# Seven-product output projections: block sums of the weights formed by accumulating loads, token operands formed beside plain tiles, reloads on another queue

## The chip, the cores and the metric

The kernel runs on one core of a Trainium2 chip. The metric is the device time of one execution in microseconds; lower is better. The matrix engine is called PE here, the vector engine DVE, the scalar engine ACT, GpSimd POOL and the sync engine SP. "POOLq" and "SPq" are the queues on which POOL and SP issue transfers.

## What is computed

One inference step of two layers over 576 tokens (64 of a running stream, 512 of a new one), model width 2048, everything in fp32. Layer A is chunk-band attention with 16 heads, layer B multi-head latent attention with 16 heads. The part that matters here is the end of each layer, an output projection of a gated mixer output, added to the layer's input:

```
y = x + (silu(gate) * mixer(rmsnorm(x))) @ w_out        # w_out is 2048 x 2048, one for each layer
```

## The kernel before

**Layout.** Activations lie transposed: 16 tiles of 128 channels by 576 tokens. For PE every fp32 operand is split into a high and a low part (`split`, L201 to L204: ACT casts the high part, DVE subtracts to get the low one), and a product is three matmuls (high·high, high·low, low·high), each with 288 tokens as its columns.

**Order of the work.** PE's instructions keep the order in which the program emits them. That order is made by `Order` (L42), which runs generators by rank and holds a clock of its own; a generator yields a pool name ("mm", "st", "x": PSUM slots) when it needs a slot. The other engines' instructions and the transfers are put in order by a scheduler that may take an instruction ahead of earlier ones when it reckons it ready. On the chip each engine and each queue then runs strictly in that order: an instruction that waits holds up all that is behind it. Tile pools are rings: the n-th tile of a pool takes the slot of the one `bufs` tiles before it, and waits until that one is done with.

**The output projection of a layer.** Its 16 tiles of 128 output channels are made in two ways. Tiles 0 to 3 are plain (`proj`, L232: 16 input tiles, 2 token halves, 3 matmuls each, so 96 matmuls; four weight parts of 128 x 512, each loaded and split by `wload`, L212). Tiles 0 and 1 are made together (`both`, L248) while the last head is still being finished; they fill the two "mm" slots of PSUM. Tiles 2 and 3 come after (`out_a` L823, `out_b` L1212); each begins when DVE has read tile 0 or 1 out of PSUM (L833 in layer A, L1222 in layer B), which adds the residual.

Tiles 4 to 15 are made in six pairs by `block_pairs` (L358). With two output tiles, two halves of the input channels (tiles 0 to 7, 8 to 15) and two token halves L and R, a two-by-two block product is done with seven products in place of eight. Each product has 24 matmuls (2 weight parts of 128 x 512, 4 blocks in each, 3 matmuls), so a pair has 168. Its weight is either a block or a sum of blocks, made by `block_weights` (L300): eight blocks of 128 x 512 are loaded by SP, and eight DVE instructions (L323, L326, L329, L333) form the sums; then `split`. Its token operand is one of the halves or a combination, made once for each layer by `block_operands` (L261): for each of eight j, four DVE subtractions (L287 to L293) and three splits on tiles j and j+8 of the mixer output. The fourth split, operand 4, overwrites the R half of the plain operand, so `last` (L295) makes it after the plain tiles. The order of the seven products is `1, 5, 6, 3, 7, 2, 4` (L361); after each one DVE adds it to the half tile of output that it belongs to (L391).

**Where the operands come from.** In layer A the mixer outputs `oA` are still on the chip. In layer B they were stored to `od` and are loaded again by 16 SP transfers (L1206 to L1209), into the same ring of 16 slots (`tag="o"`) that the raw weights of the pairs use afterwards (`raw_b`). `block_operands` is called as one piece before `out_a` and before `out_b`. After layer A each output tile is stored to `x1d`, its square is added to `lnb_acc` (`done_a`, L819; one buffer for the square), and layer B loads the tiles again by 16 SP transfers (L865 to L867) and splits them (L208, L209).

Of the kernel before, what the change touches and what calls it, by code (L numbers as in the profile page):

```python
# [15 lines left out]
F32 = mybir.dt.float32  # L16
F32R = mybir.dt.float32r
# [3 lines left out]
P = 128  # L21
D = 2048
KT = 16
# [95 lines left out]
def encoder(tc, xT, wa_in, wa_out, wb_in, wuq, wuk, wuqr, wuv, wb_out, kcT, vc, ckvcT, krcT, gains, rtab,  # L119
# [128 lines left out]
    def both(pss, name, ws, xs, before):  # L248
# [9 lines left out]
                yield None  # L258
        yield from gens[1]

    def block_operands(o, o2, pool, name):  # L261

        L, R = slice(0, 288), slice(288, 576)
        X = {1: [], 2: [], 3: [], 4: [], 5: [], 6: [], 7: []}
        for j in range(8):  # L270
            X[1].append([x[:, L] for x in o2[j]])
            X[2].append([x[:, L] for x in o2[j + 8]])
            X[3].append([x[:, R] for x in o2[j + 8]])

        def put(p, j, src):
            if p == 4:
                hi, lo = [x[:, R] for x in o2[j]]
            else:
                hi = pool.tile([P, 288], F32R, tag="T", bufs=48, name=f"{name}T{p}h{j}")
                lo = pool.tile([P, 288], F32R, tag="T", bufs=48, name=f"{name}T{p}l{j}")  # L280
            split(src, hi, lo)
            X[p].append((hi, lo))

        sub = ALU.subtract
        for j in range(8):
            a, b = o[j], o[j + 8]
            V.tensor_tensor(out=a[:, L], in0=a[:, R], in1=a[:, L], op=sub)  # L287
            put(5, j, a[:, L])
            V.tensor_tensor(out=a[:, R], in0=b[:, R], in1=a[:, R], op=sub)
            V.tensor_tensor(out=b[:, R], in0=b[:, R], in1=a[:, L], op=sub)  # L290
            put(6, j, b[:, R])
            put(7, j, a[:, R])
            V.tensor_tensor(out=b[:, L], in0=b[:, L], in1=b[:, R], op=sub)  # L293

        def last():  # L295
            for j in range(8):
                put(4, j, o[j + 8][:, L])
        return X, last

    def block_weights(w2d, pairs, seq, raw_tile, name):  # L300

        for m1, m2 in pairs:
            n_ = f"{name}{m1}"
            got, S = {}, {}

            def load(m, part):
                r = raw_tile(f"{n_}r{m}_{part}")
                nc.sync.dma_start(r, w2d[m * P:(m + 1) * P, part * WH:(part + 1) * WH])
                return r

            def block(i, k, c):
                key = i, k, c
                if key not in got:
                    got[key] = load((m1, m2)[i], 2 * k + c)
                return got[key]

            for p in seq:
                for c in range(2):
                    if p == 1:
                        src = block(0, 0, c)  # L320
                    elif p == 5:
                        S[c] = raw_tile(f"{n_}s{c}")
                        V.tensor_tensor(out=S[c], in0=block(1, 0, c), in1=block(1, 1, c), op=ALU.add)  # L323
                        src = S[c]
                    elif p == 6:
                        V.tensor_tensor(out=S[c], in0=S[c], in1=block(0, 0, c), op=ALU.subtract)  # L326
                        src = S[c]
                    elif p == 3:
                        V.tensor_tensor(out=S[c], in0=block(0, 1, c), in1=S[c], op=ALU.subtract)  # L329
                        src = S[c]  # L330
                    elif p == 7:
                        src = block(1, 0, c)
                        V.tensor_tensor(out=src, in0=block(0, 0, c), in1=src, op=ALU.subtract)  # L333
                    elif p == 2:
                        src = block(0, 1, c)
                    else:
                        src = block(1, 1, c)
                    hi = wp.tile([P, WH], F32R, tag="whi", bufs=WHL, name=f"{n_}p{p}{c}h")
                    lo = wp.tile([P, WH], F32R, tag="wlo", bufs=WHL, name=f"{n_}p{p}{c}l")
                    split(src, hi, lo)  # L340
                    yield hi, lo

    class Ahead:
        def __init__(self, gen, n):
# [10 lines left out]
            self.fill(self.n + 1)  # L355
            return self.got.pop(0)

    def block_pairs(w2d, X, pairs, raw_tile, residual, out_tile, done, name):  # L358

        L, R = slice(0, 288), slice(288, 576)  # L360
        seq = 1, 5, 6, 3, 7, 2, 4  # L361
        ws = Ahead(block_weights(w2d, pairs, seq, raw_tile, name), WHL - 2)
        for m1, m2 in pairs:
            n_ = f"{name}{m1}"
            x1, x2 = residual(m1), residual(m2)
            y1, y2 = out_tile(m1), out_tile(m2)
            yield "mm"
            a = ps_of("mm", n_ + "a")[:, 0, :288]
            bank = {1: a, 6: a, 7: a, 4: a}
            for p in seq:  # L370
                if p == 5:
                    yield "st"
                    bank[5] = bank[3] = ps_of("st", n_ + "c")[:, 0, :288]
                if p == 2:
                    yield "x"
                    bank[2] = ps_of("x", n_ + "b")[:, :288]
                for c in range(2):
                    hi, lo = ws.get()
                    for j in range(4):
                        s = slice(j * P, (j + 1) * P)  # L380
                        xh, xl = X[p][4 * c + j]
                        ends = c == 1 and j == 3
                        begins = p in (1, 2, 5) and c == 0 and j == 0
                        matmul(bank[p], hi[:, s], xh, begins, False, skip_group_check=True)
                        matmul(bank[p], hi[:, s], xl, False, False, skip_group_check=True)
                        matmul(bank[p], lo[:, s], xh, False, ends, skip_group_check=True)
                        yield None
                with tc.high_priority():
                    y, h_, add = {1: (y1, L, x1), 5: (y2, R, x2), 6: (y1, R, x1), 3: (y1, R, y1), 7: (y2, R, y2),
                                  2: (y1, L, y1), 4: (y2, L, x2)}[p]  # L390
                    V.tensor_tensor(out=y[:, h_], in0=bank[p], in1=add[:, h_], op=ALU.add)  # L391
                if p == 3:
                    od_.give("st", L_M)
                if p == 2:
                    od_.give("x", L_M)
            od_.give("mm", L_M)
            done(m1, y1)
            done(m2, y2)

# [400 lines left out]

    close(g_at)
    g_T, Tp = pool("blocksa", side="right")
    X, last_a = block_operands(oA, o2, Tp, "ao")
    g_ao, aop = pool("aout", side="right")

    def tpo(tag, dt, name):
# [16 lines left out]
    def out_a():  # L823
        for m in range(4):
            xr = residual_a(m)
            if m < 2:
                ps = first[m]
            else:
                yield "mm"
                ps = ps_of("mm", f"ao{m}")  # L830
                yield from proj(ps, wo, o2, N)
            x1 = tpo("x1", F32, f"x1_{m}")
            V.tensor_tensor(out=two(x1), in0=ps[:, :, :288], in1=two(xr), op=ALU.add)  # L833
            od_.give("mm", L_M)
            done_a(m, x1)
        last_a()
        yield from block_pairs(wa_out, X, [(m, m + 1) for m in range(4, KT, 2)], raw_a, residual_a,
                               lambda m: tpo("x1", F32, f"x1_{m}"), done_a, "ao")

    od_.spawn(5, out_a())  # L840
# [16 lines left out]

    def tpl(tag, dt, name):
        if tag == "raw":
            return lrp.tile([P, N], dt, tag=tag, bufs=RAWB, name=name)  # L860
# [342 lines left out]
    def done_b(m, y):  # L1203
        nc.gpsimd.dma_start(yT[m * P:(m + 1) * P, :], y)

    oB = []  # L1206
    for kt in range(KT):
        oB.append(bo.tile([P, N], F32, tag="o", bufs=16, name=f"bf{kt}"))
        nc.sync.dma_start(oB[kt], od[kt * P:(kt + 1) * P, :])  # L1209
    X, last_b = block_operands(oB, o2, bo, "bo")  # L1210

    def out_b():  # L1212
        for m in range(4):
# [12 lines left out]
        yield from block_pairs(wb_out, X, [(m, m + 1) for m in range(4, KT, 2)], raw_b, residual_b, out_tile_b,  # L1226
                               done_b, "bo")

    od_.spawn(5, out_b())
# [6 lines left out]

L_G, L_CQ, L_M, L_V, L_LN, L_HA, L_LB = 5.8, 10.0, 1.5, 5.0, 5.0, 8.0, 4.0
ATT = "t0 s2 t1 s3 o-1 t2 t3"
DIRECT, GA, WRAW, WHL, SGB, DEEP, VA = 2, 2, 3, 5, 2, 2, 2
LAT = (0, 1, 2, 3, 8, 4, 5, 6, 7, 9, 10)  # L1240
LAHEAD = 1
RAWB, SB, S1H, S2H, S3 = 7, 4, 3, 1, 1
# [84 lines left out]
```

## Time and profile before

| | us |
|---|---|
| median of 3 runs (2040.43 to 2044.78) | 2041.55 |
| the profiled execution | 2043.23 |
| its span | 2041.5 |
| PE busy (share of the span) | 1990.0 (97%) |
| DVE busy | 1350.7 (66%) |
| ACT busy | 1103.4 (54%) |
| POOL busy | 74.3 (4%) |
| transfers, mean over the span | 109 GB/s |

The profiled execution's own time is 1.7 us above its span and 1.7 us above the median of the runs. The pages of the profile give each engine's busy time, the waits with what ended them, tables by stretch, and the instructions in order of time. Matmuls overlap, so the time that one costs is read from how many start in a stretch, not from its own duration.

### The profile page before, as it was taken

The page shows a single profiled execution, that of the slowest core. Times are in us where ns is not written, and L with a number is a line of the kernel's source. Part 1 is how long each engine was busy: PE and PEld are TensorE (multiplying, and loading weights), DVE is VectorE, ACT ScalarE, POOL GpSimd, SP SyncE. Part 2 cuts the span into 40 slices and gives each one's busy share as a digit, 9 for nine tenths or more (in the row PEclk, how much of TensorE's full clock was granted, in tenths as well). Part 3 has the DMA queues.
Part 4 walks back from the last instruction along what each step waited for, and adds up shares of the span by engine and source line. Part 5 has one row for each costly group of instructions (what it writes and reads, how often), then busy time and mean ns, then how long its engine had stood idle before and what let it go on. Part 6 is the DMA issues. An engine that isn't in the chain of part 4 may idle for free.

```text
span 2041.5 us, 37543 instructions
## 1 busy us (share of the span) xinstructions
PE 1990.0 (97%) x14692; PEld 1969.5 (96%) x14692; DVE 1350.7 (66%) x2651; ACT 1103.4 (54%) x2034; POOL 74.3 (4%) x141
## 2 busy tenths in 40 slices
PE   8999999999999999999999899999999999995998
PEld 8999999999999999999999899999999999995998
DVE  7665555555555555558778648887776766676775
ACT  6654444544454445456344538986765656662332
POOL 0000000000000000000000000000000000000000
PEclk9999999999999999999999999999999999997999
DMA  7333333333333333333543535553223322355542
GB/s 210 86 84 94 90 85 90 83 85 89 86 94 89 86 90 78 83 81 101 171 145 118 183 78 147 159 167 112 82 77 98 86 82 84 87 154 196 164 138 68
DMA packets 121393, 223.38 MB, mean 109 GB/s; under 512 B 14272, under 2 KB 29264, under 8 KB 121216
## 3 DMA queue, kind: packets, MB, share of 16 engines
q1 hardware_dynamic: 109360, 181.22, 32.7%
q0 software_dynamic: 11856, 39.76, 5.5%
q8 instruction: 115, 1.88, 0.4%
q14 instruction: 62, 0.51, 0.1%
HBM read 183.92 MB, written 34.36 MB: 107 GB/s over the span
## 4 chain that ended last, share of the span: by engine, by line
PE 85%; issue 8%; DVE 3%; ACT 2%; DMA 1%; POOL 0%; POOLq 0%; SPq 0%; DVEq 0%; ACTq 0%
PE g L164 8%; PE lat L164 6%; PE u L164 3%; PE a2p L164 3%; PE a4p L164 3%; PE a14p L164 3%; PE a12p L164 3%; PE a9p L164 3%; PE a15p L164 3%; PE a11p L164 3%; PE a7p L164 3%; PE a8p L164 3%; PE a5p L164 3%; PE a10p L164 3%; PE a6p L164 3%
## 5 line engine op out<-in xcount | busy, mean ns | idle before, releaser
L204 DVE TENSOR_TENSOR wa_2l<-wa_2r,wa_2h 128x512 fp32r<-128x512 f32 x61 | 42.2, 691 | 92.2 <-ACT wa_2h L203 92.2
L203 ACT CAST wa_2h<-wa_2r 128x512 fp32r<-128x512 f32 x61 | 37.7, 619 | 103.7 <-PE a2p L164 10.1
L204 DVE TENSOR_TENSOR wa_3l<-wa_3r,wa_3h 128x512 fp32r<-128x512 f32 x61 | 42.2, 692 | 44.1 <-ACT wa_3h L203 42.6
L203 ACT CAST wa_0h<-wa_0r 128x512 fp32r<-128x512 f32 x61 | 37.8, 619 | 60.9 <-DMA wa_0r<-wa_in 5.2
L203 ACT CAST wa_3h<-wa_3r 128x512 fp32r<-128x512 f32 x61 | 37.7, 618 | 51.5 <-PE a2p L164 4.5
L204 DVE TENSOR_TENSOR wa_0l<-wa_0r,wa_0h 128x512 fp32r<-128x512 f32 x61 | 41.9, 687 | 17.0 <-ACT wa_0h L203 17.0
L203 ACT CAST wa_1h<-wa_1r 128x512 fp32r<-128x512 f32 x61 | 37.8, 620 | 23.7 <-PE a0pg L164 1.8
L204 DVE TENSOR_TENSOR wa_1l<-wa_1r,wa_1h 128x512 fp32r<-128x512 f32 x61 | 41.8, 685 | 10.5 <-ACT wa_1h L203 10.5
L164 PE MATMUL bo<-boh,wbo_0h 128*128 128x288 f32 x32 | 7.6, 323 | 22.4 <-DVE by L1222 22.4
L164 PE MATMUL u<-cqh,wq_0h 128*128 128x288 f32 x128 | 27.7, 298 | 0.5 <-ACT q6raw L478 0.3
L164 PEld LDWEIGHTS bo<-boh,wbo_0h 128*128 128x128 f32 x32 | 5.8, 214 | 22.6 <-issue 22.6
L164 PE MATMUL u<-cqh,wq_0l 128*128 128x288 f32 x128 | 27.4, 296 | 0.0
L164 PE MATMUL u<-cql,wq_0h 128*128 128x288 f32 x128 | 27.3, 295 | 0.0
L204 DVE TENSOR_TENSOR wb_1l<-wb_1r,wb_1h 128x512 fp32r<-128x512 f32 x25 | 17.2, 687 | 15.2 <-ACT wb_1h L203 15.1
L204 DVE TENSOR_TENSOR wb_3l<-wb_3r,wb_3h 128x512 fp32r<-128x512 f32 x25 | 17.2, 686 | 14.4 <-ACT wb_3h L203 14.3
L203 ACT CAST wb_3h<-wb_3r 128x512 fp32r<-128x512 f32 x25 | 15.4, 616 | 18.1 <-PE lat L164 9.6
L203 ACT CAST wb_1h<-wb_1r 128x512 fp32r<-128x512 f32 x25 | 15.5, 619 | 17.7 <-PE lat L164 8.8
L164 PE MATMUL lat<-bh,wb_0h 128*128 128x288 f32 x88 | 20.0, 311 | 4.5 <-ACT bh L208 4.5
L164 PE MATMUL g<-bh,wb_1h 128*128 128x288 f32 x112 | 24.3, 298 | 0.0
L164 PE MATMUL g<-bh,wb_0h 128*128 128x288 f32 x112 | 24.3, 298 | 0.0
L164 PE MATMUL g<-bh,wb_2h 128*128 128x288 f32 x112 | 24.3, 298 | 0.0
L164 PE MATMUL g<-bh,wb_3h 128*128 128x288 f32 x112 | 24.2, 298 | 0.0
(6782 smaller groups left out, 8051.9 us busy)
## 6 DMA issues: line engine op xcount, KB each, us to landing
wa_0r<-wa_in SPq DMA_DIRECT2D x61, 256.0 KB, 2.9
wa_1r<-wa_in SPq DMA_DIRECT2D x61, 256.0 KB, 2.9
wa_2r<-wa_in SPq DMA_DIRECT2D x61, 256.0 KB, 2.9
wa_3r<-wa_in SPq DMA_DIRECT2D x61, 256.0 KB, 2.9
wb_0r<-wb_in SPq DMA_DIRECT2D x25, 256.0 KB, 2.9
wb_1r<-wb_in SPq DMA_DIRECT2D x25, 256.0 KB, 2.9
wb_2r<-wb_in SPq DMA_DIRECT2D x25, 256.0 KB, 2.9
wb_3r<-wb_in SPq DMA_DIRECT2D x25, 256.0 KB, 2.9
```

The source lines that it names most:

```text
L164: nc.tensor.matmul(out, lhs, rhs, start=start, stop=stop, **kw)
L203: ACT.copy(hi, src)
L204: V.tensor_tensor(out=lo, in0=src, in1=hi.bitcast(F32), op=ALU.subtract)
```

## The change

Three things are edited, in both layers.

- **Weight sums by accumulating loads.** The DVE instructions that form sums of weight blocks are gone. A tile is loaded with one block by SP and another block is then added to it by a transfer on POOL's queue that accumulates into the tile (`accum_op=ALU.add`). Since transfers only add, signs move to the token operands (`neither`, a negated difference) and to the additions after the products (two are subtractions now). The order of the products is `5, 1, 2, 6, 4, 7, 3`. The tile of product 5 is kept: product 6 adds a block to it, product 3 another. A pair has ten plain loads and eight accumulating ones where it had eight plain ones. Loads are emitted three items ahead of the splits (`LOADS`). PSUM: products 1, 6 and 7 share an "mm" slot, 5 and 3 one "x" slot, 2 and 4 one each; "st" is no longer used here.
- **Token operands beside plain tiles.** `block_operands` returns a generator; `beside` takes one of its eight steps at every fourth step of the plain tiles 2 and 3. Each operand has a ring of its own of 16 slots (before: one of 48).
- **Reloads on POOL's queue.** The 16 loads of `x1d` at the start of layer B, and the 16 of `od` for layer B's operands, the latter in pairs (j, j+8) and five pairs ahead, go to POOL's queue.

```diff
+    def beside(gen, other, n):
+        for j, w in enumerate(gen):
+            yield w
+            if j % n == 0:
+                next(other, None)
...
+        def form():
+            for j in range(8):
+                a, b = o(j)
+                less(a[:, L], a[:, L], a[:, R])
+                put(5, j, a[:, L])
+                less(a[:, R], b[:, R], a[:, R])
+                put(7, j, a[:, R])
+                neither(b[:, R], b[:, R], a[:, L])
+                put(6, j, b[:, R])
+                neither(b[:, L], b[:, L], b[:, R])
+                late.append(b[:, L])
+                yield None
...
+    SEQ = 5, 1, 2, 6, 4, 7, 3
...
+                def add(t, src):
+                    nc.gpsimd.dma_start(t, src, accum_op=ALU.add)
...
+                        if p in (1, 7):
+                            nc.sync.dma_start(t, block(1, 1, c))
+                        elif p == 2:
+                            nc.sync.dma_start(t, block(1, 2, c))
+                        elif p == 4:
+                            nc.sync.dma_start(t, block(2, 2, c))
+                        elif p == 5:
+                            nc.sync.dma_start(t, block(2, 1, c))
+                        if p == 5:
+                            add(t, block(2, 2, c))
+                        elif p == 6:
+                            add(t, block(1, 1, c))
+                        elif p == 3:
+                            add(t, block(1, 2, c))
+                        elif p == 7:
+                            add(t, block(2, 1, c))
+                        yield t, n_
+        raws = Ahead(loads(), LOADS)
...
+                    if p == 7:
+                        V.tensor_tensor(out=two(y2), in0=two(y2), in1=ps[:, None, :].to_broadcast((P, 2, 288)),
+                                        op=ALU.subtract)
...
-                yield from proj(ps, wo, o2, N)
+                yield from beside(proj(ps, wo, o2, N), form_a, 4)
...
-        nc.sync.dma_start(x1, x1d[m * P:(m + 1) * P, :])
+        nc.gpsimd.dma_start(x1, x1d[m * P:(m + 1) * P, :])
...
-        nc.sync.dma_start(oB[kt], od[kt * P:(kt + 1) * P, :])
+            nc.gpsimd.dma_start(t[-1], od[kt * P:(kt + 1) * P, :])
...
-                yield from proj(ps, wo, o2, N)
+                yield from beside(proj(ps, wo, o2, N), form_b, 4)
```

## Rows read from the trace of the kernel before

**Rows 1.** The page, PE's busy tenths in 40 slices of 51 us.

```profile
PE   8999999999999999999999899999999999995998
```

**Rows 2.** Who PE waited for: us in total, times, longest; 850 to 1220, 1800 to 2042.

```profile
PE lat L164 <- ACT bh L208: 4.5, 1, 4.5
PE ao L164 <- DVE x L833: 4.3, 1, 4.3
...
PE bo L164 <- DVE by L1222: 22.4, 1, 22.4
```

**Rows 3.** DVE in order of time: start, us, instruction; ends of both layers' waits.

```profile
977.57 0.75 DVE L833 TENSOR_TENSOR x<-ao,xr 128x576 f32<-128x576 f32 x1
...
982.25 0.45 DVE L204 TENSOR_TENSOR aoT7l<-a7sg,aoT7h 128x288 fp32r<-128x288 f32 x1
...
1851.69 0.46 DVE L287 TENSOR_TENSOR bf<-bf 128x288 f32<-128x288 f32 x1 [4.00 <-DMA bf<-od]
...
1874.10 0.45 DVE L204 TENSOR_TENSOR boT5l<-bf,boT5h 128x288 fp32r<-128x288 f32 x1
1874.47 0.75 DVE L1222 TENSOR_TENSOR by<-bo,bxr 128x576 f32<-128x576 f32 x1
...
1876.17 0.44 DVE L204 TENSOR_TENSOR boT7l<-bf,boT7h 128x288 fp32r<-128x288 f32 x1
```

**Rows 4.** Stretches: busy us of each engine (instructions), PEclk, DMA share, GB/s.

```profile
core 0: us, PE busy (x) PEld busy (x) DVE busy (x) ACT busy (x) POOL busy (x), PEclk, DMA share, GB/s
...
974.00:978.00 4.00, 0.02 (x1) 0.00 (x0) 4.00 (x11) 2.45 (x7) 0.00 (x0) 0.94 0.08 28
978.00:982.00 4.00, 3.63 (x15) 3.63 (x16) 4.00 (x9) 2.34 (x5) 1.08 (x2) 0.50 0.65 205
982.00:990.00 8.00, 8.00 (x54) 8.00 (x53) 4.26 (x8) 1.24 (x2) 0.00 (x0) 0.85 0.66 211
...
1854.00:1866.00 12.00, 0.00 (x0) 0.00 (x0) 11.17 (x30) 4.39 (x12) 0.00 (x0) 0.67 1.05 393
...
1905.00:2035.00 130.00, 130.00 (x983) 130.00 (x982) 94.15 (x160) 48.04 (x78) 6.48 (x12) 1.00 0.40 120
```

**Rows 5.** PE in order of time, the first matmuls after layer B's wait.

```profile
1875.36 0.82 PE L164 MATMUL bo<-boh,wbo_0h 128*128 128x288 f32 x2 [22.44 <-DVE by L1222]
...
1880.09 0.42 PE L164 MATMUL bo<-boh,wbo_1h 128*128 128x288 f32 x2
```

**Rows 6.** SP's queue in order of time, raw weights of layer B's first pair.

```profile
1861.53 5.99 SPq L308 DMA_DIRECT2D bo4r<-wb_out  x4
...
1891.64 1.13 SPq L308 DMA_DIRECT2D bo4r<-wb_out  x2
```

**Rows 7.** Transfers by tile: queue, count, KB each, median us to landing.

```profile
bf<-od SPq DMA_DIRECT2D x16, 288.0 KB, 6.0
...
bo8r<-wb_out SPq DMA_DIRECT2D x8, 256.0 KB, 3.1
...
b15qf<-qd POOLq DMA_DIRECT2D x1, 288.0 KB, 4.1
```

**Rows 8.** The page's groups: a weight split; busy us, mean ns, idle before.

```profile
L204 DVE TENSOR_TENSOR wb_1l<-wb_1r,wb_1h 128x512 fp32r<-128x512 f32 x25 | 17.2, 687 | 15.2 <-ACT wb_1h L203 15.1
...
L203 ACT CAST wb_1h<-wb_1r 128x512 fp32r<-128x512 f32 x25 | 15.5, 619 | 17.7 <-PE lat L164 8.8
```

**Rows 9.** POOL in order of time: the store that ends a pair, two pairs of layer B.

```profile
1948.20 0.54 POOL L1204 DMA_DIRECT2D yT<-by  x1 [2.79 <-DVE by L391]
...
1970.47 0.54 POOL L1204 DMA_DIRECT2D yT<-by  x1 [2.91 <-DVE by L391]
```

**Rows 10.** ACT and DVE in order of time, between layer A's last product and layer B.

```profile
1141.95 0.68 ACT L406 ACTIVATE lnb15sq<-x 128x576 f32<-128x576 f32 x1 [2.57 <-DVE x L391]
...
1142.67 0.76 DVE L407 TENSOR_TENSOR lnb_acc<-lnb_acc,lnb15sq 128x576 f32<-128x576 f32 x1 [0.81 <-ACT lnb15sq L406]
...
1146.05 0.81 DVE L209 SCALAR_TENSOR_TENSOR bl<-bx,gn,bh 128x576 fp32r<-128x576 f32 x1
```

More of the change, by code (lines that the diff above doesn't have):

```diff
@@ L278, in put, with less @@
             else:
-                hi = pool.tile([P, 288], F32R, tag="T", bufs=48, name=f"{name}T{p}h{j}")
-                lo = pool.tile([P, 288], F32R, tag="T", bufs=48, name=f"{name}T{p}l{j}")
+                hi = pool.tile([P, 288], F32R, tag=f"T{p}", bufs=16, name=f"{name}T{p}h{j}")
+                lo = pool.tile([P, 288], F32R, tag=f"T{p}", bufs=16, name=f"{name}T{p}l{j}")
             split(src, hi, lo)
             X[p].append((hi, lo))
[L284 to L293, printed above, removed]
+        def less(out, a, b):
+            V.tensor_tensor(out=out, in0=a, in1=b, op=ALU.subtract)
@@ new lines, in neither @@
+        def neither(out, a, b):
+            V.scalar_tensor_tensor(out=out, in0=a, scalar=-1.0, in1=b, op0=ALU.mult, op1=ALU.subtract)
+        def form():
[10 more added lines that the diff above has]
+                yield None
@@ L295, in last @@
         def last():
             for j in range(8):
[L297 to L341, printed above, removed]
@@ new lines, in last, with block_weights, loads, block @@
+                put(4, j, late[j])
+        late = []
+        return X, form(), last
+    SEQ = 5, 1, 2, 6, 4, 7, 3
+    def block_weights(w2d, pairs, raw_tile, sum_tile, name):
+        def loads():
+            for m1, m2 in pairs:
+                S = {}
+                def block(i, k, c):
+                    m, part = (m1, m2)[i - 1], 2 * k - 2 + c
+                    return w2d[m * P:(m + 1) * P, part * WH:(part + 1) * WH]
+                def add(t, src):
+                    nc.gpsimd.dma_start(t, src, accum_op=ALU.add)
+                for p in SEQ:
+                    for c in range(2):
+                        n_ = f"{name}{m1}p{p}{c}"
+                        if p == 5:
+                            t = S[c] = sum_tile(n_)
+                        elif p in (6, 3):
+                            t = S[c]
+                        else:
+                            t = raw_tile(n_)
+                        if p in (1, 7):
[6 more added lines that the diff above has]
+                            nc.sync.dma_start(t, block(2, 1, c))
+                        if p == 5:
+                            add(t, block(2, 2, c))
[7 more added lines that the diff above has]
+        raws = Ahead(loads(), LOADS)
+        for _ in range(14 * len(pairs)):
+            src, n_ = raws.get()
+            hi = wp.tile([P, WH], F32R, tag="whi", bufs=WHL, name=n_ + "h")
+            lo = wp.tile([P, WH], F32R, tag="wlo", bufs=WHL, name=n_ + "l")
+            split(src, hi, lo)
+            yield hi, lo
@@ L836, in out_a @@
         last_a()
-        yield from block_pairs(wa_out, X, [(m, m + 1) for m in range(4, KT, 2)], raw_a, residual_a,
+        yield from block_pairs(wa_out, X, [(m, m + 1) for m in range(4, KT, 2)], raw_a, raw_a, residual_a,
                                lambda m: tpo("x1", F32, f"x1_{m}"), done_a, "ao")
@@ L859, in tpl @@
         if tag == "raw":
-            return lrp.tile([P, N], dt, tag=tag, bufs=RAWB, name=name)
+            return lrp.tile([P, N], dt, tag="raw", bufs=RAWB, name=name)
         bufs = {"s1": SB, "s2": SB, "s3": S3}.get(tag, 1)
@@ L1204, in done_b, with pair_b @@
         nc.gpsimd.dma_start(yT[m * P:(m + 1) * P, :], y)
-    oB = []
-    for kt in range(KT):
-        oB.append(bo.tile([P, N], F32, tag="o", bufs=16, name=f"bf{kt}"))
-        nc.sync.dma_start(oB[kt], od[kt * P:(kt + 1) * P, :])
-    X, last_b = block_operands(oB, o2, bo, "bo")
+    def pair_b(j):
+        t = []
+        for kt in (j, j + 8):
+            t.append(bo.tile([P, N], F32, tag="o", bufs=16, name=f"bf{kt}"))
+            nc.gpsimd.dma_start(t[-1], od[kt * P:(kt + 1) * P, :])
+        return t
+    oB = Ahead((pair_b(j) for j in range(8)), 5)
+    X, form_b, last_b = block_operands(lambda j: oB.get(), o2, bo, "bo")
     def out_b():
@@ L1225, in out_b @@
         last_b()
-        yield from block_pairs(wb_out, X, [(m, m + 1) for m in range(4, KT, 2)], raw_b, residual_b, out_tile_b,
+        yield from block_pairs(wb_out, X, [(m, m + 1) for m in range(4, KT, 2)], raw_b, raw_b, residual_b, out_tile_b,
                                done_b, "bo")
```

50 lines of the change are left out of this document (25 added, 25 removed).

## Prediction, made before the change was run

> **What bounds the kernel now.** I read the slices first: PE is at nine tenths or more nearly everywhere, and a stretch of slices near the end falls to five [rows 1]. A gain can therefore come only from PE's few gaps, or from fewer matmuls, and the change keeps all matmuls. The list of PE's waits gives the gaps: 4.3 us in layer A and 22.4 us in layer B, both ended by the DVE addition that reads plain tile 0 out of PSUM, and 4.5 us at the start of layer B's projections [rows 2]. The instructions in order of time say why that addition was late: DVE was running `block_operands`. In layer B its first subtraction waits for reloaded tiles and starts at 1851.7, the addition (L1222) comes at 1874.5, with only two of the piece's instructions behind it; in layer A the addition (L833) comes at 977.6 in the midst of the same work, which ends at 982.7 [rows 3]. After each gap PE runs at the lower clock: granted 0.50 in 978 to 982 and 0.85 in 982 to 990 [rows 4]. Within the pairs there is nothing to gain: 130.00 of 130 us busy, 983 matmuls, so 0.132 us each, while DVE has 36 us free [rows 4]. A change of 0.2%, about 4 us, is what a measurement of this kernel can tell from none.
>
> **The change part by part.**
>
> *Operands beside the plain tiles.* The additions L833 and L1222 are now emitted before the first step of the operands, so they no longer stand behind them; what they need is the residual and PE's result. Both gaps go: 4.3 + 22.4 = 26.7 us. With them goes the slow restart. Layer A: 69 matmuls start in 978 to 990, PE idle for 0.4 us of it; at 0.132 us the other 11.6 us hold 88, so 19 are missing, 2.5 us. Layer B: from 1875.36 to 1880.09 are 24 matmuls in 4.73 us [rows 5], against 3.2, so 1.5 us. Together 30.7 us.
>
> What is late next is DVE. A layer's operands are 8 x 7 = 56 DVE instructions, which start 0.37 us apart (1874.10 to 1874.47 [rows 3]): 20.7 us. Plain tiles 2 and 3 take PE 2 x 96 x 0.132 = 25.4 us. DVE also has to split their weights and to make two additions of some 0.67 us. In layer A the work is begun early and ends 5 us after the gap's end [rows 3], some 17 us before the first pair now: cover enough, cost 0 (2 at worst). In layer B the tiles land at about 1851 as now; POOL's queue is free to issue them when the last head is stored, and the loads run at the transfer engines' full rate, 393 GB/s at a share of 1.05 [rows 4], whichever queue issues them. 20.7 us of operands, 4 splits [rows 8] and 4 additions (some 5 us) end at about 1877, and the first pair starts at 1852.9 + 25.4 = 1878.3 (the wait that ends at 1875.36 began 22.44 us earlier [rows 5]). That just fits.
>
> *A slot in layer B's ring that is late.* `pair_b` takes slots in the order j, j+8, so the second raw weight tile (product 5, part 1) falls on the slot of tile 8, which `last` must have read first. Its read can't come before plain tile 3 is past its first step (about 1866), and perhaps only after the operands (1877). In the kernel before, the two loads with such slots were issued 30 us after the first four [rows 6]; they belonged to a late product then. Now a load (3.1 us [rows 7]), an accumulating load (4 to 5, an estimate from the 4.1 us of a plain POOL load [rows 7]) and a split (0.62 + 0.69 and a handover, 1.4 [rows 8]) follow, 9 us, and PE wants it 1.6 us into the pair, at 1880. So 0 to 6 us of waiting, and at the far end a slow restart of 1.5: I take 4.5 in all, as DVE will be full until 1877.
>
> *Weight sums by transfers.* 8 DVE instructions for each pair go; in the pairs DVE isn't the bound [rows 4], so they give 0. Eight loads become ten, and eight accumulating ones come in. No row shows one. Its cost to the engines: at least a plain load, 256 KB at 393 GB/s = 0.67 us; at most, I say, three passes (load, read the tile, write it through), 2.0 us. A pair takes 1970.47 - 1948.20 = 22.27 us [rows 9]. Ten plain loads and four residuals and outputs of 288 KB are 3.80 MB, 9.7 us. That leaves 12.6 us for eight, 1.57 us each. At one pass the engines are at 68%, at two (1.33 us) at 92%, at three at 115%. I take two passes, a load plus a read of the tile, which lies midway: hidden, cost 0; ends 0 and +41 us (12 pairs x 8 x 0.43). A gain is excluded, as PE has no gap in the pairs.
>
> By the Trainium skill (Collectives: The Full Stack, The bandwidth ceiling: the fold count and why AG ≠ RS ≠ AR) an add in a transfer is slower than a copy because it reads two sources, about half the rate. No run here shows it yet; by it the eight take 10.7 us, the sum stays as it is, and 1.9 us of each pair are left as margin.
>
> The latency has cover too. A sum tile passes from one accumulating load to a split to the next load, with six items of 12 matmuls, 9.5 us, between uses. A link is 0.54 us of issue on POOL [rows 9], the landing (4.1 us for a plain POOL load, 6.0 in the crowded burst [rows 7]) and 1.4 us of split: 6 to 8 us. The first one of a pair may stand behind the stores of the outputs before it, some 1.5 us more: 9.5 at the worst end. Cost 0, at the edge. What waits behind a late one: the splits on ACT and DVE, the additions (L391) on DVE, then PE.
>
> *New order of products, banks, two-sided addition.* Banks are read with another product (3.2 us) between as now; the wider addition of product 7 is 0.3 us more and nothing waits for it. Sixteen negated differences for each layer cost DVE some 0.03 us more each (0.81 against 0.75 for 576 columns [rows 3, 10]). Cost 0.
>
> *From layer A to B.* The path there is the last addition, a square, the sum `lnb_acc`, its split, then the first operand [rows 10]. The last product belonged to the second tile of the pair; now product 3 is last and belongs to the first, while the sum runs in the order first, second, with one buffer for the square. So a square and an addition, 0.68 + 0.76 us [rows 10], are added on the path: +1.5. The reloads of `x1d` move from SP to POOL, past the two last stores of layer A; most were loaded ahead before, and I expect the same. SP's weights come sooner, but wait for nothing. Cost 0, from -3 to +3.
>
> **The sum**, against the profiled execution's own 2043.2 us: -26.7 - 4.0 + 4.5 + 1.5 = -24.7, so 2018.5. The median of the runs shown is 1.7 us lower than that execution, within their spread; I round up to 2019.
>
> **The rivals.**
>
> *A, slower: the accumulating loads fill the transfer engines.* The place is the pairs' loads. If one takes over 1.57 us of the engines, pairs stretch by eight times the excess; at 1.57 + 24.7 / 96 = 1.83 us the gain is gone. At three passes it is 2018.5 + 41 = 2060. For it: no row shows the operation, and the share rises from 0.40 [rows 4] to near full at two passes. Against it: 393 GB/s is what the engines carried in a burst, so two passes fit.
>
> *B, about as before: latency.* If an accumulating load lands in 8 us rather than 4 to 5, each of two links in a pair is late by 0.5 to 1.5 us: 12 x 1 to 12 x 2 us, 2031 to 2043. For it: the crowded burst had 6.0 us [rows 7], and POOL's queue holds loads behind stores that wait for PE. Against it: at the rate of the pairs plain loads land in 3.1.
>
> *C, less gain: DVE becomes the bound beside the plain tiles.* The work just fits in layer B; if weight splits for tile 3 stand behind operand steps that wait for reloads, 5 to 12 us come back: 2024 to 2031.
>
> That the change doesn't do what it says has no good case: the order of the two additions against the operands is plain in the program.
>
> **How the numbers follow.** Forecast (2011 to 2024) 0.50, C 0.15, B 0.17, A 0.18. The likeliest gives 2019. Downward the limit is no give-back at all, 2043.2 - 30.7 = 2012.5, and the spread of runs: 2010. Upward the range takes in B and the lower part of A: 2046, leaving out about 0.15 above and 0.03 below. Faster: 0.50 + 0.15 + two thirds of B = 0.76; within 0.2%: the rest of B and a little of A, 0.07; slower: 0.17.
>
> **What would show it.** Right: no PE wait on L833 or L1222; clock 1.00 through plain tiles 2 and 3; in the pairs 0.132 us a matmul with a transfer share of 0.8 to 1.0; a wait of a few us on a weight split in layer B's first pair. Two passes or three is read from the share in the pairs. Wrong: PE waiting for product 6's or 3's split in every pair (A if the share is at its ceiling, B if it is not), or DVE full and PE waiting on `wbo` splits in tile 3 (C).

## The result and the profile after

The changed kernel takes 2078.2 us (median of 4 runs, 2074.2 to 2080.7) against 2042.0 (4 runs, 2040.4 to 2044.8): ratio 1.0174, 95% interval 1.0153 to 1.0196, so 36 us slower. The forecast was 2019 us, with a range of 2010 to 2046.

The page of after, PE's and the transfer engines' tenths in 40 slices of 52 us:

```profile
PE   8999999999999999999988799999999999998888
...
DMA  7233333333333333325897635563233323358985
```

The hole of tile 2 [rows 1] is gone. In its place PE is a little short in the slices of the pairs (20 and 21, 36 to 39, counted from 0), and there the transfer engines stand at 7 to 9, the last slice apart. PE's waits in 850 to 1250, then in 1800 to 2080 (us in total, times, longest):

```profile
PE lat L164 <- ACT bh L208: 9.6, 1, 9.6
PE ao4a L164 <- DVE x L424: 3.6, 1, 3.6
PE ao12a L164 <- DVE x L424: 2.8, 1, 2.8
PE ao8p L164 <- ACT ao8p31h L203: 2.6, 1, 2.6
...
PE bo4a L164 <- DVE by L424: 5.3, 1, 5.3
PE bo4p L164 <- DVE bo4p50l L204: 5.1, 1, 5.1
PE bo L164 <- DVE by L1259: 3.6, 1, 3.6
PE bo10p L164 <- ACT bo10p31h L203: 2.7, 1, 2.7
```

Of the two gaps [rows 2] the one in layer A has no successor, and the one in layer B (L1259 now) is 3.6 us in place of 22.4. New are waits in the pairs: for the split of product 3's sum (`p31h`; pairs 6, 8 and 10 of both layers, a pair going by its first output tile) and for an output addition (L424). The wait into layer B's projections has doubled. Two stretches of layer A's pairs (columns as in [rows 4]), the second in its last pair, after:

```profile
1030.00:1110.00 80.00, 67.97 (x489) 65.03 (x489) 36.21 (x64) 26.08 (x46) 22.25 (x27) 1.00 0.88 214
1137.00:1158.00 21.00, 21.00 (x161) 21.00 (x160) 13.24 (x24) 9.40 (x16) 6.71 (x12) 1.00 0.67 174
```

In the 80 us 489 matmuls start; the kernel before has 599 there at a transfer share of 0.48. By PE's first matmuls a pair took 22.2 to 22.8 us before. Now layer A's six take 28.6, 27.1, 27.6, 27.5, 26.8 and 22.4, layer B's 37.5, 24.2, 27.9, 27.1, 24.5 and 22.4: the last pair of a layer, which has no next pair's loads beside it, loses nothing. Landings in the same view as [rows 7], after:

```profile
xr<-xT SPq DMA_DIRECT2D x16, 288.0 KB, 5.2
x1d<-x POOLq DMA_DIRECT2D x16, 288.0 KB, 7.8
...
ao8p<-wa_out SPq DMA_DIRECT2D x10, 256.0 KB, 7.8
...
ao8p<-wa_out POOLq DMA_DIRECT2D x8, 256.0 KB, 7.5
...
bo8p<-wb_out POOLq DMA_DIRECT2D x8, 256.0 KB, 7.8
```

Before, the residuals and stores (`xr`, `x1d`) land in 3.3 and 3.4 us and the weights of the pairs in 3.1 to 4.5. Past each layer's first pair the plain weights now take 6.7 to 7.8 us by pair (once 9.7), and layer A's stores 7.8: about twice as long.

From PE's first and last instructions by tile the span divides into stages. The table has the profiled executions of before, after and four experiments told below (us; "wait" is PE's wait for layer B's first operand):

| | before | after | e2 plain second | h1 no chain | h2 fewer plain | f1 beside only |
|---|---|---|---|---|---|---|
| start to layer A's pairs | 1006.7 | 998.9 | 999.5 | 999.7 | 1000.4 | 999.2 |
| layer A's pairs | 134.7 | 160.0 | 133.7 | 145.7 | 142.2 | 134.2 |
| wait | 4.5 | 9.6 | 10.1 | 9.4 | 8.5 | 4.5 |
| to layer B's pairs | 756.6 | 740.0 | 738.6 | 736.4 | 736.8 | 733.2 |
| layer B's pairs to the end | 139.0 | 169.7 | 150.2 | 162.5 | 159.4 | 148.2 |
| span | 2041.5 | 2078.2 | 2032.1 | 2053.7 | 2047.3 | 2019.3 |

After against before: -7.8, +25.3, +5.1, -16.6, +30.7. The gaps gave 24 us, and the pairs took back more than twice as much.

### The profile page after: what moved, and what is told of

It reads as the page before. It is cut to its first block, busy times and chain, and to the rows that moved or that the text cites. A ratio compares the mean times of both kernels' runs of the same rounds, so it can differ in the third digit from the quotient of the medians.

```text
span 2078.2 us, 37755 instructions
## 1 busy us (share of the span) xinstructions
PE 2005.8 (97%) x14692; PEld 1979.3 (95%) x14692; DVE 1289.2 (62%) x2555; ACT 1099.9 (53%) x2034; POOL 176.8 (9%) x269
## 4 chain that ended last, share of the span: by engine, by line
PE 81%; DMA 10%; DVE 3%; issue 2%; ACT 2%; POOL 1%; POOLq 0%; SPq 0%; DVEq 0%; ACTq 0%
PE g L164 8%; PE lat L164 7%; PE u L164 3%; PE a2p L164 2%; PE ao L164 2%; PE a5p L164 2%; PE a7p L164 2%; PE a14p L164 2%; PE a13p L164 2%; PE a12p L164 2%; PE a10p L164 2%; PE a15p L164 2%; PE a6p L164 2%; PE a4p L164 2%; PE a11p L164 2%; PE a9p L164 2%
## 5 line engine op out<-in xcount | busy, mean ns | idle before, releaser
L203 ACT CAST wa_2h<-wa_2r 128x512 fp32r<-128x512 f32 x61 | 37.7, 619 | 103.7 <-PE a2p L164 10.1
L164 PE MATMUL lat<-bh,wb_0h 128*128 128x288 f32 x88 | 20.0, 311 | 9.6 <-ACT bh L208 9.6
L164 PE MATMUL u<-cqh,wq_0h 128*128 128x288 f32 x128 | 27.7, 298 | 0.5 <-ACT q6raw L510 0.3
L164 PE MATMUL u<-cqh,wq_0l 128*128 128x288 f32 x128 | 27.4, 296 | 0.0
L164 PE MATMUL u<-cql,wq_0h 128*128 128x288 f32 x128 | 27.4, 295 | 0.0
L164 PEld LDWEIGHTS lat<-bh,wb_0h 128*128 128x128 f32 x88 | 15.1, 201 | 9.9 <-ACT bh L208 9.9
L164 PE MATMUL g<-bh,wb_1h 128*128 128x288 f32 x112 | 24.3, 298 | 0.0
L164 PE MATMUL g<-bh,wb_0h 128*128 128x288 f32 x112 | 24.3, 298 | 0.0
L164 PE MATMUL g<-bh,wb_2h 128*128 128x288 f32 x112 | 24.3, 298 | 0.0
L204 DVE TENSOR_TENSOR wb_2l<-wb_2r,wb_2h 128x512 fp32r<-128x512 f32 x25 | 17.1, 685 | 11.4 <-ACT wb_2h L203 11.4
L164 PE MATMUL g<-bh,wb_3h 128*128 128x288 f32 x112 | 24.2, 298 | 0.0
```

Source lines behind the costliest of these rows:

```text
L164: nc.tensor.matmul(out, lhs, rhs, start=start, stop=stop, **kw)
L203: ACT.copy(hi, src)
L204: V.tensor_tensor(out=lo, in0=src, in1=hi.bitcast(F32), op=ALU.subtract)
```

## The experiments

A single time is that of one execution; where an interval stands, the kernels were executed several times. The kernel before took 2042 to 2043 us beside them (medians).

### What the accumulation costs: e2, e3, e5

```diff
-                    nc.gpsimd.dma_start(t, src, accum_op=ALU.add)
+                    nc.gpsimd.dma_start(t, src)                                   # e2
+                    nc.gpsimd.dma_start(t[:64, :], src[:64, :], accum_op=ALU.add) # e3
+                    nc.gpsimd.dma_start(t[:96, :], src[:96, :], accum_op=ALU.add) # e5
```

> The eight accumulating loads of a pair become plain loads into the same tiles on the same queue with the same waits, so the sums are left out and the output is another. Theory 1 (an accumulating load takes the transfer engines more than a plain one, and they are full): the pairs go back to about 22.3 us, time 2020 to 2030. Theory 2 (POOL's queue holds the loads of product 3 behind those of the next pair's product 5, which wait for a landing): the order stays, so most of the loss stays, 2050 or more.

> Each accumulating load adds only to 64 of the 128 partitions, so half of each added block is left out. Theory 1: the engines' work in the pairs falls by about a quarter and nearly the whole loss goes, 2020 to 2035. Theory 2 (order on the queue and a fixed latency): the landing gets somewhat shorter but the order stays, 2045 to 2065.

> The kernel after the change with each accumulating load cut to 96 of its 128 partitions, so that a quarter of every second block is left out of the sums. Theory, the transfer engines are full: by the shares read, a pair's ten plain loads, two residuals and two stores take about 10.0 us of all engines and an accumulating load of three quarters about 1.18, so 19.4 us of the 22.3 that PE needs, 87 per cent: nothing stretches, 2034 to 2040 us, with a share of 0.85 to 0.90 in the pairs. Rival, each accumulating load costs by its size wherever the share stands (latency and order on POOL's queue): half of the way from 2034 to 2079, so 2050 to 2062 us, with the share below 0.85.

Measured: e2 2033.9, e3 2034.4, e5 2053.2 us, after 2078.2. So the accumulation costs 44 us, half of its bytes next to nothing (0.5 us; the pairs of e3 take 4 us longer than those of e2, other stages less), and three quarters 19. The loss sets in between, but not where the engines' time for a pair runs out: e5 was to need 87 per cent and lose nothing. The same 80 us of e2, e3 and e5, a fence for each:

```profile
1030.00:1110.00 80.00, 80.00 (x606) 80.00 (x606) 50.65 (x82) 35.25 (x57) 18.32 (x35) 1.00 0.75 247
```

```profile
1030.00:1110.00 80.00, 79.46 (x600) 79.26 (x600) 47.40 (x83) 33.23 (x56) 26.67 (x34) 1.00 0.78 196
```

```profile
1030.00:1110.00 80.00, 72.64 (x528) 69.96 (x526) 41.97 (x74) 30.24 (x52) 22.98 (x30) 1.00 0.85 217
```

PE is full at a share of 0.75, all but full at 0.78 and short at 0.85. What grows with the share is the landing. The slowest POOL load of a pair in this stretch (`ao8p`) is in each kernel product 3's second sum, or the plain load in its place. The landings of that pair's POOL loads in e2, e3, e5 and after the change:

```profile
DMA to landing us min/median/max: 3.6/4.5/5.9
DMA to landing us min/median/max: 5.0/6.1/7.1
DMA to landing us min/median/max: 4.3/6.7/9.0
DMA to landing us min/median/max: 5.4/7.5/11.5
```

The prediction's cover of 9.5 us for a link, less 0.5 of issue and 1.4 of split, leaves 7.6 for the landing: in this pair e2 and e3 are below it, e5 and the changed kernel above. (In other pairs of e3 the same load takes up to 8.9 us and PE doesn't wait for it, so the mark is a rough one.) e5's time lies in the range of its rival, latency and order on POOL's queue. GB/s doesn't tell how full the engines are here: e5 moves fewer bytes than e2 at a higher share.

### An accumulating load by itself: m1

The kernel holds nothing but bursts of 128 x 512 loads (`src(i)` is a block of `wa_in`), and single loads that wait for each other:

```diff
+    for i in range(n):
+        nc.gpsimd.dma_start(b[i], src(40 + i), accum_op=ALU.add)
...
+    for i in range(8):
+        V.tensor_copy(q[i][:, 0:1], last[:, 1:2])
+        nc.gpsimd.dma_start(q[i], src(108 + i), accum_op=ALU.add)
+        last = q[i]
```

> The whole computation is left out. Five stretches of transfers into tiles of 128 x 512, each stretch begun when the one before has landed: 20 plain loads on SP, 20 plain on POOL, 20 accumulating on POOL, a mix of 20 plain on SP with 16 accumulating on POOL, then single loads on POOL that each wait for the one before, 8 plain and 8 accumulating. By the rows of before a plain load in a burst takes 0.67 us of all engines. Prediction's term: an accumulating load takes 1.33 us, so the third stretch lasts about 27 us against 13. Reading of the pairs after the change (shares of 0.85 to 0.90 at 26 to 27 us a pair): 1.6 to 1.9 us, so 32 to 38 us. Latency alone: if the operation itself is slow, a single accumulating load lands in 6 us or more; if only the crowd makes it late, in under 5, within 1.5 us of a plain one.

The view by stretches (us, DVE busy, POOL busy, PEclk, share, GB/s): the middle of the burst of 20 accumulating loads, and of the mix of 20 plain with 16 accumulating ones:

```profile
44.00:60.00 16.00, 0.00 (x0) 12.60 (x15) 1.00 1.12 197
76.00:100.00 24.00, 0.00 (x0) 8.68 (x11) 1.00 1.09 255
```

262,144 bytes at 197 GB/s are 1.33 us: the prediction's two passes, and half of the 393 GB/s of plain loads [rows 4]. By the Trainium skill (Collectives: The Full Stack, The bandwidth ceiling: the fold count and why AG ≠ RS ≠ AR) an add reads two sources and runs at about half the rate; this burst agrees. The mix takes the sum of its parts: in its middle an accumulating load of POOL's queue and a plain one of SP's land in turn, and POOL issues the next when one has landed:

```profile
83.56 0.86 POOL L153 DMA_DIRECT2D sp<-wa_in  x1 [1.16 <-DMA sp<-wa_in]
...
91.56 0.86 POOL L153 DMA_DIRECT2D sp<-wa_in  x1 [1.16 <-DMA sp<-wa_in]
```

These are four steps in 8.0 us, 2.0 us each, as 1.33 + 0.67 make. Single loads on POOL, plain (L160) and accumulating (L164), where each starts when the one before has landed, with their issue and the view's line of landings for either:

```profile
135.04 0.54 POOL L160 DMA_DIRECT2D one<-wa_in  x1 [2.85 <-DVE one L159]
DMA to landing us min/median/max: 2.6/2.7/2.8
...
162.70 0.86 POOL L164 DMA_DIRECT2D one<-wa_in  x1 [3.12 <-DVE one L163]
DMA to landing us min/median/max: 3.4/3.5/3.6
```

From the start of its issue a plain one lands in 2.7 us and an accumulating one in 3.5; 0.3 of the difference is POOL's longer issue (0.86 against 0.54). So alone it is not slow: the 7.5 to 8.6 us of most pairs are made by what runs beside it and ahead of it. My reading of 1.6 to 1.9 us of engine time from the pairs' shares falls: a share in a crowd is no price.

### The chain, or the crowd: h1, h2

```diff
                         elif p in (6, 3):
-                            t = S[c]
+                            t = old.get((p, c), S[c])     # h1: tiles of products 2 and 4, one pair ago
...
+                        elif p in (2, 4):                 # h2: product 1's tiles, no load
+                            t = S[c, 1]
```

> The kernel after the change, but from the second pair on products 6 and 3 add their blocks not to the sum of product 5 but to tiles of the pair before, split long ago (so those weights are wrong). Every transfer stays, in number, size and queue; the links sum, split, next sum are gone. Theory, the chain (rival B of the prediction, with a landing of 8 us in place of 4 to 5): PE stops waiting for product 6's and 3's splits and most of the 44 us come back, 2034 to 2048 us. Rival, full engines: the transfers are the same and so is the loss, 2065 to 2080, with the share in the pairs at 0.85 to 0.90.

> The kernel after the change without the plain loads of products 2 and 4, whose weights are taken from product 1's tiles instead (so they are wrong): 4 of a pair's 10 plain loads are left out, all accumulating loads and their links stay. By the burst's rows a pair then needs 6 x 0.67 + 4 x 0.75 + 8 x 1.39 = 18.1 us of the engines in 22.3, 81 per cent in place of 93. Theory, full engines: the accumulating loads land in 6 us or so and the loss is mostly gone, 2034 to 2048 us. Rival, an accumulating load is late whatever else is carried (its own 1.39 us, the two tiles of a product together, POOL's order): landings stay near 8 us and the time above 2060.

Measured: h1 2055.5, h2 2049.1 us: h1 between the two ranges expected and h2 just above the first, so neither theory holds alone. Without the links sum, split, next sum, and with as many transfers of the same size on the same queues, 23 of the 44 us come back; PE's waits for `p31h` and `p30h` are gone. (The order of the sums on POOL's queue is another too, as they wait for other tiles.) What is left in h1 are mostly waits for output additions, and a share that reaches 1.00:

```profile
1030.00:1110.00 80.00, 76.59 (x573) 75.77 (x571) 46.59 (x79) 34.92 (x57) 26.58 (x33) 1.00 1.00 253
```

The chain of waits of h1 in that stretch says why such an addition (L428 there) is late: another one ahead of it in DVE's queue waits for the store that frees its output tile, 7.9 us on its way.

```profile
1030.37 7.86 DMA x1d<-x
1038.23 0.03 DVEq L428
1038.26 0.17 DVE ao6p60l L204
1038.43 0.14 issue
1038.57 0.69 DVE ao6p61l L204
1039.26 0.38 DVE x L428
```

In h2 29 us come back with all links in place, at a share of 0.82 in the same stretch. Yet accumulating loads of the pair `ao8p` still land in 7.5 us there (median), as the rival said, while past the first pairs PE waits for no split of a sum, only for output additions. The 23 and 29 us make more than the 44, so the two causes overlap: links with little room, and loads that arrive late. After's own chain of waits, with POOL's issues and one of DVE's instructions from there, shows how they meet, between layer A's third and fourth pair:

```profile
1057.51 8.03 DMA ao10p<-wa_out
...
1063.86 0.46 DVE L424 TENSOR_TENSOR x<-xr,ao8p 128x288 f32<-128x288 f32 x1 [3.96 <-DMA x1d<-x]
...
1066.12 0.90 POOL L331 DMA_DIRECT2D ao10p<-wa_out  x1 [8.37 <-DVE x L424]
1066.68 1.24 POOL L331 DMA_DIRECT2D ao8p<-wa_out  x1
1067.24 1.57 POOL L331 DMA_DIRECT2D ao10p<-wa_out  x1
1067.78 1.91 POOL L331 DMA_DIRECT2D ao8p<-wa_out  x1
...
1067.78 11.45 DMA ao8p<-wa_out
1079.33 0.63 ACT ao8p31h L203
```

Product 6's splits of this pair (`ao8p`), on which product 3's sums depend, stand on DVE behind an addition that waits for a store. That store stands in POOL's queue behind the two sums of product 6 and lands 1.1 us after them. Then POOL stands at a sum of the next pair (`ao10p`, its product 7), which waits for a plain load of 8.0 us. Behind it come product 3's first sum of this pair, product 7's second and product 3's second. They land in this order, 2.0 to 3.1 us apart, so that the last lands 11.4 us after its issue where the first took 5.5. So the scheduler's order on POOL's queue has a part in how late that load is: two sums that PE doesn't want yet land ahead of one that it waits for. What this costs is not shown: no run moves them, or the stores to another queue. How the 44 us divide among links, landings, POOL's order and the few output tiles is not told apart by these runs.

### How far ahead loads are emitted: e4, e7

```diff
-DIRECT, GA, WRAW, WHL, SGB, DEEP, VA, LOADS = 2, 2, 3, 5, 2, 2, 2, 3
+DIRECT, GA, WRAW, WHL, SGB, DEEP, VA, LOADS = 2, 2, 3, 5, 2, 2, 2, 1   # e4; 5 in e7
```

> LOADS from 3 to 1: loads are emitted one item ahead of the splits, so the next pair's loads come later in the order. Theory 1: no gain, 2075 to 2090. Theory 2: the loads of product 3 are no longer behind the next pair's, and the pairs fall towards 23 to 24 us, 2040 to 2060.

> The kernel after the change with LOADS 5 in place of 3: loads and accumulating loads are emitted five items ahead of the splits, so the product-5 sums of the next pair come further ahead of their use. Theory, full engines: the work for the engines is the same, 2070 to 2080 us, as LOADS 1 gave 2079. Rival, latency: the two links with room gain 2 items of 1.6 us each, so several us of a pair come back, 2045 to 2060.

Measured: 2079.2 and 2076.9 us. Emitting earlier or later doesn't help: on POOL's queue product 7's sums of the next pair still stand between product 3's, the second of which lands 11.8 us after its issue in both (the same pair), and the plain loads that POOL waits for are as late.

### The crowd without accumulation: e6

```diff
-                    nc.gpsimd.dma_start(t, src, accum_op=ALU.add)
+                    nc.gpsimd.dma_start(t, src)
+                    nc.sync.dma_start(next(spare), w2d[m1 * P:(m1 + 1) * P, 0:768])
```

> The kernel after the change with every accumulating load made a plain one, as in e2_plain_second (so that no block is added and the sums are wrong), and for each one a copy of 384 KB between places in DRAM, on SP's queue, that nothing waits for. Waits and their order are those of the kernel after; the accumulation is gone, the transfer engines are as full as with it, or fuller (16 us of a pair for the loads and outputs plus 8 copies). Theory, full engines: the loads land later and the time goes from 2034 back to 2065 or more, with a share of 0.85 or more in the pairs. Rival, the accumulation's own latency in the chain from sum to split to sum: no more than 2034 to 2042, though the share is as high.

Measured: 2063.9 us, and no answer. The copies wait for nothing, so the scheduler put all 96 of them ahead, at 36 to 218 us (PE's tiles of layer A's pairs come 33 us later than in e2, and their stretch is as long as there). The time comes near the theory's, but for another reason.

### The rest of the change without accumulation: e1

```diff
-                    nc.gpsimd.dma_start(t, src, accum_op=ALU.add)
...
+            def sum_of(out, x, y):
+                V.tensor_tensor(out=out, in0=x, in1=y, op=ALU.add)
+                return out
```

> The changed kernel with the sums of weight blocks formed on DVE again (eight plain loads and eight DVE additions for each pair, same order of products, same signs, same operands beside plain tiles, same reloads on POOL). If the accumulating loads are the whole loss, by whichever mechanism, the pairs go back to 22.3 us and the forecast's sum stands: about 2019 (2015 to 2028, as the start of layer B now waits 9.6 us). If the moved operands or the moved reloads lose time by themselves it stays above 2035.

Measured: 2047.5 us, ratio 1.0014 (1.0002 to 1.0026). All other parts together, with the sums back on DVE, don't gain either: PE waits 1.4 to 2.4 us in three pairs of layer A for output additions, which stand in DVE's queue behind sums of the next pair that wait for their loads, 8.6 us into layer B, 3.5 at layer B's tile 2, and 4.7 in its first pair. One such sum, 5 us ahead of a late addition, with no idle time of DVE over 0.1 us between:

```profile
1074.39 0.69 DVE L335 TENSOR_TENSOR ao12r<-ao12r,ao12r 128x512 f32<-128x512 f32 x1 [2.31 <-DMA ao12r<-wa_out]
...
1079.72 0.45 DVE L413 TENSOR_TENSOR x<-xr,ao10a 128x288 f32<-128x288 f32 x1
```

### One part alone: f1, and where its reloads go: f2, f3

f1 is the kernel before (signs, product order, DVE sums, 48-slot ring) with `beside`, a `form()` of the old steps, and the lazy reloads of `od`. f2 and f3 change one queue each:

```diff
-        nc.sync.dma_start(x1, x1d[m * P:(m + 1) * P, :])
+        nc.gpsimd.dma_start(x1, x1d[m * P:(m + 1) * P, :])               # f2
...
-            nc.gpsimd.dma_start(tB[kt], od[kt * P:(kt + 1) * P, :])
+            nc.sync.dma_start(tB[kt], od[kt * P:(kt + 1) * P, :])         # f3
```

> The kernel before with one part of the change alone: the token operands are formed beside plain tiles 2 and 3, and layer B's operand tiles are reloaded in pairs on POOL's queue. Sums stay on DVE, the order of the products, the signs, the operands' ring and the slots of the 16 tiles are those of before; x1d is reloaded on SP as before. My theory: both gaps of PE go (4.3 + 22.4 us) with most of the slow restarts (4.0), and nothing of the rest of the change is there to take it back; the second raw weight tile of layer B's first pair falls on the slot of tile 1 here, which no late operand reads, so that pair isn't held up: 2012 to 2018 us. Rival, DVE full beside the plain tiles: the first pair of layer B still takes 30 us or more in place of 22 (it took 32 with plain second loads), because 56 operand instructions stand among its weight splits: 2022 to 2027 us.

> The kernel of f1_beside_only with one more part of the change: the 16 loads of x1d at the start of layer B are issued on POOL's queue. After the change PE waits 9.6 us there for the first operand, before 4.5. Theory, the reloads on POOL: they start earlier, beside SP's weights and the load of the cached rope keys, whose landing (7.9 us) holds up ACT's queue ahead of the first operand; so here the wait is 8 to 10 us again and the time 4 to 5 us over f1_beside_only. Rival, the order of the products (a further square and addition after product 3): the wait stays at 4 to 5 us, and the time within 1 us of f1_beside_only.

> The kernel of f1_beside_only with the lazy reloads of od on SP's queue in place of POOL's. Theory of the prediction (the queue that issues them doesn't matter, the last head's store and the engines' rate do): within 2 us of f1_beside_only, and PE waits of the same size at the plain tiles. Rival: on SP the reloads wait for the last head's store with the weights and residuals of the plain tiles behind them in the same queue, so PE waits for wbo splits there, 4 to 10 us more than f1_beside_only.

Measured: f1 2019.9 us, ratio 0.9889 (0.9875 to 0.9904); f2 2026.9, 0.9926 (0.9909 to 0.9942); f3 2018.5, 0.9885 (0.9871 to 0.9900). This part alone beats both kernels. Both gaps are gone and the wait into layer B is the old one; PE's waits of f1 in 850 to 1240 and in 1800 to 2055:

```profile
PE lat L164 <- ACT bh L208: 4.5, 1, 4.5
...
PE bo4a L164 <- DVE bo4p10l L204: 5.3, 1, 5.3
```

The second is the rival of f1's expectation, DVE full beside the plain tiles (the rival C of the prediction): with the lower clock that PE is granted after this wait (0.50 in 1875 to 1880) the first pair takes 30.8 us in place of 22.2, as the rival said, though the time is below its range. The split of product 1's weight was cast at 1861.2 and got its turn on DVE at 1876.1, behind the eight splits of operand 4 (`bol`):

```profile
1872.84 1.92 DVE L204 TENSOR_TENSOR bol<-bf,boh 128x288 fp32r<-128x288 f32 x5
...
1876.08 0.68 DVE L204 TENSOR_TENSOR bo4p10l<-bo4r,bo4p10h 128x512 fp32r<-128x512 f32 x1
```

f2 costs 7.0 us more than f1, and its chain of waits tells why for 4.5 of them:

```profile
1133.17 0.33 SPq L217
1133.50 0.05 issue
1133.55 7.57 DMA krc<-krcT
1141.12 0.02 issue
1141.14 0.30 ACT KRh L203
1141.44 0.69 ACT bh L208
```

With the reloads on POOL the cached rope keys (`krc`) are still on their way when layer B starts, and ACT's cast of them stands in order ahead of the first operand: the wait is 9.0 us, as after the change (there `krc` takes 7.9 us). In f1 that cast isn't what the operand waits for. f3 against f1 is within both intervals: no difference between the queues that reload `od` is shown.

### Late operand splits after the first product: g1

```diff
+                if p == 1 and late:
+                    late()
+                    late = None
...
-        last_b()
```

> The kernel of f1_beside_only with the eight late splits of layer B's operand 4 emitted after the first product of the first pair in place of before it, which nothing needs until the seventh product. In f1_beside_only PE waits 5.3 us there for the weight split of the first product, which stands in DVE's queue behind operand steps and these splits. Theory (DVE full beside the plain tiles): eight splits of 0.37 us, 3 us, leave the path, and the wait falls to about 2: 2016 to 2018 us. Rival: the weight split stays behind the operand steps, which the scheduler has put first, and nothing is gained: 2019 to 2020.

Measured: 2017.8 us, ratio 0.9877 (0.9861 to 0.9894). The wait for `bo4p10l` falls from 5.3 to 1.6 us, as expected; 2.1 us of time are within the spread, so only the wait is shown:

```profile
PE bo4a L164 <- DVE bo4p10l L204: 1.6, 1, 1.6
```

## Why the prediction was wrong

**Operands beside the plain tiles: right.** The terms were 6.8 us in layer A and 23.9 in layer B. f1, which makes this edit alone (with the reloads of `od`), has 7.5 and 23.4. In the changed kernel layer A gave 7.8, layer B 16.6: a residual (`bxr`) that lands in 8.2 us among the reloads leaves 3.6 us of the gap, with a granted clock of 0.83 in 1875 to 1885 behind it.

**Weight sums by transfers: the step that failed.** It had two halves. The engine time was right: two passes, 1.33 us measured, so 20.4 us of engines for a pair of 22.3. The latency was not: I took 4 to 5 us for a landing, from rows of an emptier machine, and called a link of 6 to 8 us against 9.5 of cover "at the edge". In nine of the twelve pairs the sums land in 7.5 to 8.6 us (medians; 5.5 to 9.6 in all), so that a link is about 10 with issue and split, and a pair's last sum in up to 11.5. h1, without the links and with another order on POOL's queue, takes 22.7 us less. Rival B put down 12 to 24 for the links; its own two links, late by 0.5 to 1.5 us each, make 12 to 36. By the prediction's own sign, waits for product 3's splits (in half of the pairs) with the share below its ceiling, it is B that came. The prediction then priced only the links. At nine tenths of the engines, stores that free output tiles and residuals land late as well, and POOL's queue holds one pair's sum behind another's: the other 21.6 us (h1 against e2) had no term in the sum, and how they divide is open. Room in the mean (1.9 us of a pair) was taken for cost 0; e5, with less to carry, already loses 19 us. The room was smaller, too: h1's pairs in the 80 us above take 23.5 us each at a share of 1.00, which at the mix's 1.09 would be 21.5 us of the engines, 0.8 below PE's 22.3 (an estimate from these rows). Rival A came nearest in size (2060 at three passes), for a cause that m1 excludes.

**Layer B's first pair: under-sized.** I put down 4.5 us for the late slot. Products 5 and 6 wait 5.1 and 5.3 us in the changed kernel, 3.9 and 2.9 in e2, where nothing accumulates; the whole pair, 22.2 us before, takes 37.5 and 32.3. In f1, which has no late slot there, the same place costs 5.3 through DVE and the pair takes 30.8, so f1 too loses 8.6 us here; the two causes I kept apart, a late slot and rival C, share one place. My account of DVE (20.7 us of operands and 5 of the rest, "that just fits") left out the eight splits of operand 4, 3.0 us at 0.37 each, which stand ahead of the first pair's splits; g1 moves them and the wait falls by 3.7 us.

**From layer A to B: the wrong term.** I charged 1.5 us for a square and a sum more, and nothing for the reloads on POOL. The wait grew by 5.1 us, and f2, with the old order of products, shows 4.5 of them to be the reloads' (7.0 us in all); the square and the sum have little left (0.6 here, 1.1 in e2). The bound of -3 to +3 was too narrow.

**New order of the products:** 0 in the pairs when the second loads are plain (layer A's pairs 133.7 us in e2 against 134.7), as forecast.

## What to carry to other kernels

Work that moves from an engine to the transfer engines needs room in their latency, not only in their mean: here next to nothing was lost at a share of 0.78, and 19 and 44 us at 0.85 and 0.88. Before a chain of transfers is given a cover, take its landing time from the most crowded row there is, ask what stands ahead of it in its queue, and list everything else in that stretch that waits for a landing. When a change has several parts, time each alone: here one edit is worth 23 us and the others cost 58.

## What was not expected of the hardware

An accumulating load costs POOL 0.86 us to issue against 0.54, two plain loads' worth of the engines, and shows in GB/s as one load. Alone it lands only 0.8 us later than a plain one (3.5 against 2.7 from the start of its issue); among others, at a share of 0.88, it takes 7.5 to 8.6 us in most pairs, and a plain load of the weights 6.7 to 7.8 against 3.1 to 4.5 before. Four such loads issued within 1.7 us on one queue landed one behind another, 2.0 to 3.1 us apart.
